# Drawn offsets on the priorities of two mixers, and a memset in place of a transfer of zeros

## The chip, the cores and the metric

The kernel runs on one core of a Trainium2 chip. The metric is the device time of one execution in microseconds; the median of the runs counts. Five engines work side by side, each through its own instructions in order: TensorE (PE in the profile; PEld are its weight loads), VectorE (DVE), ScalarE (ACT), GpSimd (POOL) and SyncE (SP), which here issues the transfers.

## The reference

Two layers of a model of width 1024 run on one sequence of 256 tokens. Each layer is feed-forward, mixer, feed-forward, each followed by a layer norm over the scaled residual:

```python
for layer in range(DEPTH):
    i = layer // 2
    h = layer_norm(DEEPNORM_ALPHA * h + 0.5 * swiglu(h, ffn_w_in[layer, 0], ffn_w_out[layer, 0]), ...)
    if layer % 2 == 0:
        mix = hybrid_mixer(h, ...)
    else:
        mix = nsa_mixer(h, positions, ...)
    h = layer_norm(DEEPNORM_ALPHA * h + mix, ...)
    h = layer_norm(DEEPNORM_ALPHA * h + 0.5 * swiglu(h, ffn_w_in[layer, 1], ffn_w_out[layer, 1]), ...)
```

`hybrid_mixer` projects the tokens and runs two branches: a gated delta rule with 8 value heads, whose chunks need the solution of a triangular system, and a state space scan with 16 heads; both are gated, normalised and projected back. `nsa_mixer` is attention with 16 heads in 2 groups, over compressed, selected and windowed keys.

## The kernel before

The kernel is first written down as a plan and then ordered. Every call such as `nc.vector.tensor_tensor` appends an operation to `self.plan.ops` (`Plan.add`), with the tiles that it reads and writes, its dependences on earlier operations (two accesses of one PSUM bank of which one writes are always kept in order) and a priority: its place in the list, `op.prio = op.idx + self.base`. `Plan.order` then walks through time with a list of ready operations for each engine. On each engine it takes the operation that can start first by prices written out in `Plan.price`, and among those that could start at once the one of lowest priority. Tiles are given their buffers as they are first written; there are two "ps" banks, two "mp" banks and four "acc" banks of PSUM, four "raw" buffers for arriving weights, and 36 tiles of 128x1024 floats for the rest. `K.copy` leaves it to this walk whether ACT or DVE makes a copy. `Plan.emit` issues the operations in the order found, which is why every line of the profile is L534, the line that emits.

Float32 products are made of three matmuls of a rounded kind: a weight tile `raw` is split into a rounded part `whi` and the rest `wlo` (`split`), and `mm3` multiplies high by high, high by low and low by high. Weight splits are most of the work of DVE and much of that of ACT. Small products, transposes (against `ident`) and the inverse run as plain float32 matmuls.

The six stages (feed-forward, hybrid, feed-forward, feed-forward, NSA, feed-forward) are planned one after the other in `run`. Inside the hybrid stage five generators are woven by `weave`, which always continues the one that has made least progress by planned PE time: `delta` (the delta rule and its inverse), `space` (convolutions), `gate`, `space2` (the scan) and `out_a` (the output projection of the first half). The NSA stage weaves `attention`, `dense` (projections of queries, keys and values), `compressed` and `out_g0`. So the place of an operation in the list is the place at which its generator was continued.

The inverse of the triangular system is in `delta`. Sixteen chunk matrices of 64x64 a half partition are inverted by levels: the diagonal blocks of 16 rows by VectorE (`sw`, `Ab`, `W`), then level 4 joins them to blocks of 32 and level 5 to blocks of 64. For a level, `X` times `AT` is masked and written to the columns `half(Tt, 0)` of the tile T (`Tt`, 16 matrices of 64 columns a partition); `Y` and T give the products that are subtracted from `Y` and `X`. At level 4 `half(Tt, 0)` are columns 0 to 15 and 32 to 47 of each 64, at level 5 columns 0 to 31. The products read all 64 columns of T, so between the levels columns 32 to 47 have to be zero again. `zero` does that for the whole tile with a transfer from a tile of zeros, issued on SyncE:

```python
self.nc.sync.dma_start(H3(t, n), self.zeros[:, None, :].to_broadcast([P, n, P]))
```

T and the two `Y` tiles are also cleared this way once ahead of the levels.

Of the kernel before, what the change touches and what calls it, by code (L numbers as in the profile page):

```python
# [40 lines left out]
NSA_SB = (("acc",), ("acc",), ("ps",), ("ps",))  # L41
CATCH = 1
ZERO_AT = 8

ENDS = 3

# [6 lines left out]
def H3(t, h):  # L53
    return t.rearrange("p (h t) -> p h t", h=h)
# [503 lines left out]
class K:  # L558
# [556 lines left out]
    def hybrid(self, x, then):  # L1115
        self.arena = None
        nc, i = self.nc, self.i
# [97 lines left out]
        for n, src in enumerate((kT, qT)):  # L1215
            sq = H3(self.m4(1024, "sq"), 4)
            nc.scalar.activation(sq, src, AF.Square)
            for h in range(4):
                o, c = n * 4 + h, h % 2
# [29 lines left out]
        def delta():  # L1249
# [40 lines left out]
            for j in range(15):  # L1290
# [3 lines left out]
                V.tensor_tensor(W[:, j + 1:, :j + 1], W[:, j + 1:, :j + 1], u, OP.subtract)  # L1294
                if j == ZERO_AT:
                    late = _Gate(self.plan, len(self.plan.ops) - 1)
# [5 lines left out]
            X, Tt = (H3(self.m4(1024, n, "D"), 16) for n in ("X", "T"))  # L1302
# [19 lines left out]
            for lev in (4, 5):  # L1322
                n = 1 << lev
                nb = 32 // n
                half = lambda t, q: t.rearrange("p h (j two i) -> p h j two i", two=2, i=n)[:, :, :, q, :]
                packed = lambda ps: ps.rearrange("p (h j i) -> p h j i", j=nb, i=n)
                m = lm[:, lev - 4, :].rearrange("p (j i) -> p j i", i=n)
                yield
                pT = self.bank("acc")
                for b, h, cp, k in heads:  # L1330
                    nc.tensor.matmul(pT[cp, k * 32:(k + 1) * 32], AT[b][cp, h, cp], half(X, 0)[cp, k], start=True, stop=True)
                V.tensor_tensor(half(Tt, 0), packed(pT), m[:, None].to_broadcast([P, 16, nb, n]), OP.mult)
                yield
                pX, pY = self.bank("acc"), self.bank("acc")
                for b, h, cp, k in heads:
                    nc.tensor.matmul(pY[cp, k * 32:(k + 1) * 32], Tt[cp, k, :], half(Ys[b][cp, :, cp], 1)[:, h],
                                     start=True, stop=True)
                for b, h, cp, k in heads:
                    nc.tensor.matmul(pX[cp, k * 32:(k + 1) * 32], Ys[b][cp, h, cp], half(Tt, 0)[cp, k], start=True, stop=True)
                for b, Y in enumerate(Ys):  # L1340
                    for cp in CP:
                        y = half(Y[cp, :, cp], 1)
                        V.tensor_tensor(y, y, packed(pY[cp, b * 256:(b + 1) * 256]), OP.subtract)
                V.tensor_tensor(half(X, 0), half(X, 0), packed(pX), OP.subtract)
                if lev < 5:
                    self.zero(Tt)

            yield
            pT = [self.bank("acc") for b in range(2)]
# [59 lines left out]
            for b, d in enumerate(blk):  # L1409
                tb = slice(b * P, (b + 1) * P)  # L1410
                attnT, vn = d['attnT'], d['vn']
                o = H3(self.m4(1024, f"o{b}"), 8)
# [138 lines left out]
        def out_a():  # L1551
# [3 lines left out]
            for s in range(4):  # L1555
                wo = self.unit_rows(w_out, 2 * s, 2, 0, D)
                for e in range(2):
                    for b in range(2):
                        for c in range(2):
                            cs = slice(c * 512, (c + 1) * 512)  # L1560
                            self.mm3(acc[b][c], self.xb(oT[0], b, 2 * s + e), (wo[e][0][:, cs], wo[e][1][:, cs]),
                                     s + e == 0, False)
                        yield
        self.weave(list(zip((delta(), space(), gate(), space2(), out_a()), W_HYB)))
        terms = []
        for s in range(4):
# [420 lines left out]
    def run(self, stages):  # L1987
        nc = self.nc
        self.ah = [None, None]
        self.first = True  # L1990
        x = self.new_x()

        warm = self.bank("acc")

        def spin(*heads):
            for n in heads:
                nc.tensor.matmul(warm[:, :n * P], self.ones, self.ones[:, None, :].to_broadcast([P, n, P]),
                                 start=True, stop=True)

        tab = self.one([P, 1], "tab")  # L2000
        nc.scalar.activation(tab, self.mhalf, AF.Silu)
        spin(4, 2)
        self.ah = [self.m4(D, f"h{b}", "L") for b in range(2)]

        def load(b, q):
            cs = slice(q * 512, (q + 1) * 512)
            nc.sync.dma_start(self.ah[b][:, cs], self.i['x'][0, b * P:(b + 1) * P, cs])
            self.transpose_half(x, b, self.ah[b], q)

        load(0, 0)  # L2010
        with _Gate(self.plan, len(self.plan.ops) - 3):
            spin(2, 2)
        self.arrivals = [[], [lambda: load(1, 0)], [], [lambda: load(0, 1), lambda: load(1, 1)]]
        for n, (kind, l, j, idx) in enumerate(stages):
            last = n == len(stages) - 1
            state = {}

            def then(b, acc, s, state=state, last=last, l=l, idx=idx):
                if b == 0:
                    state['x'] = None if last else self.new_x()  # L2020
                    state['gb'] = self.ln_params(l, idx)
                self.layer_norm(b, acc, s, state['gb'], state['x'], last)
            if kind == 'ffn':
                self.ffn(l, j, x, lambda b, acc: then(b, acc, 0.5), last)
            elif kind == 'hyb':
                self.hybrid(x, lambda b, acc: then(b, acc, 1.0))
            else:
                self.nsa(x, lambda b, acc: then(b, acc, 1.0))
            x = state['x']


STAGES = [('ffn', 0, 0, 0), ('hyb', 0, 0, 1), ('ffn', 0, 1, 2), ('ffn', 1, 0, 0), ('nsa', 1, 0, 1), ('ffn', 1, 1, 2)]
# [37 lines left out]
```

## Time and profile before

| what | value |
|---|---|
| median of 3 runs | 1120.43 us (1120.2 to 1120.77) |
| profiled execution | 1120.57 us |
| its span, first to last instruction | 1118.5 us |
| granted TensorE clock | 0.998 |
| PE / PEld / DVE / ACT / POOL busy | 99% / 84% / 79% / 46% / 5% of the span |
| TensorE matmuls | 6545 |
| read from HBM | 194.04 MB, 174 GB/s over the span |

A row of instructions in a timeline reads: start, duration, engine, line, operation, output tile <- input tiles, shapes, count, and in brackets the idle time of the engine ahead of it with what ended it. "Issue" stands for an engine that waited for nothing that the profile shows. Matmuls overlap, and their ends are modelled, so a busy PE is not PE at its peak.

### The profile page before, as it was taken

The page shows a single profiled execution, that of the slowest core. Times are in us where ns is not written, and L with a number is a line of the kernel's source. Part 1 is how long each engine was busy: PE and PEld are TensorE (multiplying, and loading weights), DVE is VectorE, ACT ScalarE, POOL GpSimd, SP SyncE. Part 2 cuts the span into 40 slices and gives each one's busy share as a digit, 9 for nine tenths or more (in the row PEclk, how much of TensorE's full clock was granted, in tenths as well). Part 3 has the DMA queues.
Part 4 walks back from the last instruction along what each step waited for, and adds up shares of the span by engine and source line. Part 5 has one row for each costly group of instructions (what it writes and reads, how often), then busy time and mean ns, then how long its engine had stood idle before and what let it go on. Part 6 is the DMA issues. An engine that isn't in the chain of part 4 may idle for free.

```text
span 1118.5 us, 16483 instructions
## 1 busy us (share of the span) xinstructions
PE 1105.6 (99%) x6545; PEld 943.9 (84%) x6545; DVE 888.5 (79%) x1494; ACT 516.6 (46%) x930; POOL 56.3 (5%) x104
## 2 busy tenths in 40 slices
PE   9999999999999999999999999999999999999997
PEld 7888888899999788888888888888887678888886
DVE  6977768799979999777767977876879989777765
ACT  4635332278736545533423633433346776333320
POOL 1000000012001410000000000000000000000000
PEclk9999999999999999999999999999999999999999
DMA  9876562642933276755564665655426237755511
GB/s 335 302 252 199 183 219 80 188 133 55 271 114 105 85 241 211 263 188 188 189 192 146 236 213 184 201 182 164 150 71 232 76 113 248 242 188 195 181 39 38
DMA packets 148886, 198.37 MB, mean 177 GB/s; under 512 B 9389, under 2 KB 123722, under 8 KB 148810
## 3 DMA queue, kind: packets, MB, share of 16 engines
q1 hardware_dynamic: 148810, 197.33, 53.5%
q8 instruction: 51, 0.84, 0.3%
q14 instruction: 25, 0.20, 0.1%
HBM read 194.04 MB, written 1.05 MB: 174 GB/s over the span
## 4 chain that ended last, share of the span: by engine, by line
PE 87%; DVE 7%; ACT 2%; issue 2%; DMA 1%; POOL 1%; SPq 0%; DVEq 0%; ACTq 0%; POOLq 0%
PE ps L534 52%; PE acc L534 31%; PE mp L534 5%; DVE wlo L534 2%; DVE cv L534 1%; DVE arena L534 1%; DMA raw<-in_nsa_w_in_dram 1%; DVE o L534 0%; POOL arena L534 0%; DMA raw<-in_ffn_w_in_dram 0%; DVE AT L534 0%; ACT P L534 0%; DVE whi L534 0%; DVE y L534 0%; DVE qs L534 0%
## 5 line engine op out<-in xcount | busy, mean ns | idle before, releaser
L534 DVE TENSOR_TENSOR wlo<-raw,whi 128x1024 fp32r<-128x1024 f32 (+2 forms) x351 | 416.3, 1207 | 10.9 <-ACT whi L534 7.7
L534 PE MATMUL ps<-x,whi 128*128 128x512 f32 (+2 forms) x1584 | 369.1, 363 | 1.4 <-ACT cv L534 1.0
L534 PEld LDWEIGHTS ps<-x,whi 128*128 128x128 f32 (+1 forms) x1584 | 278.6, 188 | 46.1 <-ACT cv L534 2.9
L534 ACT ACTIVATE whi<-raw 128x1024 fp32r<-128x1024 f32 (+2 forms) x258 | 258.4, 1045 | 28.2 <-DMA raw<-in_ffn_w_in_dram 17.6
L534 PE MATMUL acc<-whi,g 128*128 128x512 f32 x698 | 228.4, 391 | 0.0
L534 PE MATMUL ps<-x,wlo 128*128 128x256 f32 x1368 | 222.4, 283 | 0.0
L534 ACT ACTIVATE sg<-ps 128x256 f32<-128x256 f32 x156 | 60.0, 385 | 343.4 <-PE ps L534 343.4
L534 PEld LDWEIGHTS ps<-x,wlo 128*128 128x128 f32 x1368 | 197.6, 190 | 11.3
L534 DVE TENSOR_TENSOR sg<-ps,sg 128x256 f32<-128x256 f32 (+1 forms) x158 | 67.4, 427 | 155.6 <-ACT sg L534 154.9
L534 PEld LDWEIGHTS acc<-whi,g 128*128 128x128 f32 x698 | 131.4, 188 | 25.8
L534 PE MATMUL acc<-wlo,g 128*128 128x512 f32 x349 | 136.9, 392 | 0.0
L534 PE MATMUL ps<-whi,x 128*128 128x512 f32 (+1 forms) x480 | 128.6, 385 | 0.0
L534 PEld LDWEIGHTS ps<-whi,x 128*128 128x128 f32 x480 | 85.7, 188 | 15.3 <-issue 0.8
L534 PEld LDWEIGHTS acc<-wlo,g 128*128 128x128 f32 x349 | 65.8, 189 | 10.8
L534 PE MATMUL acc<-whi,x 128*128 128x512 f32 x224 | 74.6, 405 | 0.3 <-DVE x L534 0.2
L534 PE MATMUL ps<-wlo,x 128*128 128x512 f32 (+1 forms) x240 | 67.2, 380 | 0.0
L534 DVE CAST whi<-raw 128x1024 fp32r<-128x1024 f32 (+2 forms) x93 | 63.4, 682 | 4.0 <-DMA raw<-in_nsa_w_in_dram 4.0
L534 PEld LDWEIGHTS acc<-whi,x 128*128 128x128 f32 x224 | 41.6, 188 | 10.3 <-DVE x L534 1.0
L534 PEld LDWEIGHTS ps<-wlo,x 128*128 128x128 f32 x240 | 43.3, 188 | 7.1
L534 POOL TENSOR_TENSOR lnve<-lnve,mhalf 128x1 f32<-128x1 f32 x12 | 11.5, 956 | 735.5 <-DVE lnve L534 735.5
L534 ACT ACTIVATE sg<-sg 128x256 f32<-128x256 f32 x72 | 30.2, 419 | 33.3 <-DVE sg L534 33.1
L534 PE MATMUL acc<-wlo,x 128*128 128x512 f32 x112 | 42.9, 398 | 0.0
(251 smaller groups left out, 1013.1 us busy)
## 6 DMA issues: line engine op xcount, KB each, us to landing
raw<-in_ffn_w_in_dram SPq DMA_DIRECT2D x72, 1024.0 KB, 5.1
raw<-in_ffn_w_out_dram SPq DMA_DIRECT2D x44, 1024.0 KB, 5.1
raw<-in_hyb_w_in_dram SPq DMA_DIRECT2D x20, 1024.0 KB, 5.3
raw<-in_ffn_w_in_dram SPq DMA_DIRECT2D x30, 512.0 KB, 4.9
raw<-in_hyb_w_out_dram SPq DMA_DIRECT2D x8, 1024.0 KB, 5.1
raw<-in_nsa_w_in_dram SPq DMA_DIRECT2D x5, 1024.0 KB, 5.6
raw<-in_nsa_cmp_w_dram SPq DMA_DIRECT2D x4, 1024.0 KB, 5.5
raw<-in_nsa_w_out_dram SPq DMA_DIRECT2D x4, 1024.0 KB, 6.1
```

Source lines behind the costliest of these rows:

```text
L534: r = getattr(getattr(nc, eng), fn)(*[res(a) for a in args], **{k: res(a) for k, a in kw.items()})
```

## The change

A table `ORDER` names two stages, 1 (hybrid) and 4 (NSA), with a seed number, a spread and a run length. `run` notes at which operation each stage begins. After all stages are planned, the operations of those two stages get an offset on their priority: each run of eight consecutive operations shares one draw from a normal distribution, times 3.0. The offsets act in `Plan.order` alone; the list, the dependences and the work stay. Between levels 4 and 5 of the inverse, the transfer over all of T gives way to a memset on GpSimd over columns 32 to 47 of each matrix.

```diff
+ORDER = {
+    1: [(38, 3.0, 8)],
+    4: [(180, 3.0, 8)],
+}
...
                 if lev < 5:
-                    self.zero(Tt)
+
+                    nc.gpsimd.memset(half(Tt, 0)[:, :, 1], 0.0)
...
+        self.marks = []
         for n, (kind, l, j, idx) in enumerate(stages):
+            self.marks.append(len(self.plan.ops))
...
+        ends = self.marks[1:] + [len(self.plan.ops)]
+        for n, terms in ORDER.items():
+            a, e = self.marks[n], ends[n]
+            for number, spread, run in terms:
+                off = np.random.default_rng(number * 10 + n).standard_normal((e - a) // run + 2)
+                for o in range(a, e):
+                    self.plan.ops[o].prio += spread * off[(o - a) // run]
```

## The prediction

> **What bounds the kernel now.** I read the page's shares first, then busy time by stretch, then the waits of TensorE, then the timeline around its holes.
>
> ```profile
> span 1118.5 us, 16483 instructions
> ## 1 busy us (share of the span) xinstructions
> PE 1105.6 (99%) x6545; PEld 943.9 (84%) x6545; DVE 888.5 (79%) x1494; ACT 516.6 (46%) x930; POOL 56.3 (5%) x104
> ```
>
> TensorE (PE) is without work for 1118.5 - 1105.6 = 12.9 us in all. The profiled execution took 1120.57 us, 2.07 us more than its span; the median of the runs, 1120.43, is 0.14 us below it. The three runs differ by 0.57 us; I count 0.2%, 2.24 us, as about what a measurement of this kernel can tell from no change.
>
> Busy time by stretch puts the idle time into stages (columns: busy PE, PEld, DVE, ACT, POOL, then granted clock, DMA share, GB/s). 187 to 460 us is about the first mixer, 794 to 970 the second, 460 to 609 the inside of a feed-forward stage.
>
> ```profile
> 187.00:460.00 273.00, 271.47 (x2056) 240.35 (x2055) 250.22 (x467) 154.49 (x242) 38.10 (x52) 1.00 0.50 159
> 460.00:609.00 149.00, 149.00 (x784) 128.28 (x783) 105.57 (x159) 53.72 (x87) 0.00 (x0) 1.00 0.58 192
> ...
> 794.00:970.00 176.00, 173.75 (x1057) 138.62 (x1056) 151.84 (x276) 108.33 (x277) 10.49 (x26) 1.00 0.48 162
> ```
>
> The feed-forward stretch has no idle PE at all. The mixers, the only stages whose priorities are drawn anew, have 273.00 - 271.47 = 1.53 us and 176.00 - 173.75 = 2.25 us: 3.78 us together. The clock is 1.00 throughout, so no order can gain clock. The rest of the 12.9 us lies at the start and the end of the program, out of the change's reach.
>
> The waits of PE name the holes (who waited for whom: us in total, times, longest):
>
> ```profile
> PE ps L534 <- ACT q L534: 1.3, 1, 1.3
> PE acc L534 <- POOL ones L534: 1.1, 1, 1.1
> PE ps L534 <- ACT cv L534: 1.0, 1, 1.0
> PE mp L534 <- ACT P L534: 0.5, 1, 0.5
> PE mp L534 <- DVE q L534: 0.4, 1, 0.4
> PE mp L534 <- DVE x L534: 0.3, 1, 0.3
> ```
>
> The wait for `ones` is the program's start. The other five lie in the mixers, each happens once, and they add up to 1.3 + 1.0 + 0.5 + 0.4 + 0.3 = 3.5 of the 3.78 us. Each is an accident of order, not a rate that is too low, as the two large ones show. The first, in the hybrid mixer:
>
> ```profile
> 270.90 1.29 ACT L534 ACTIVATE sw<-AT 32x256 f32<-32x256 f32 x2
> ...
> 272.21 0.38 ACT L534 ACTIVATE cv<-ps 128x256 f32<-128x256 f32 x1
> 272.49 0.59 ACT L534 ACTIVATE zs<-ps 128x512 f32<-128x512 f32 x1
> 272.65 0.30 PEld L534 LDWEIGHTS ps<-x,whi 128*128 128x128 f32 x2 [1.46 <-ACT cv L534]
> ```
>
> Two copies that gather the inverse's diagonal blocks stand on ACT ahead of the copy that empties a projection bank; both "ps" banks are full, and PE waits. Had the `cv` copy gone first, it would have run 1.29 us earlier, more than the hole. The second, in the NSA mixer:
>
> ```profile
> 871.55 0.51 ACT L534 ACTIVATE P<-acc,arena 128x256 f32<-128x256 f32 x1
> ...
> 872.00 0.64 ACT L534 ACTIVATE q<-ps 128x512 f32<-128x512 f32 x1
> ...
> 872.69 0.19 PEld L534 LDWEIGHTS ps<-fixed 128*128 128x128 f32 x1 [1.52 <-ACT q L534]
> ```
>
> Here the copy of the queries that empties the bank stands behind the attention's exponentials, and frees it at 872.64, just before PE goes on.
>
> **The change, part by part.** *The T edit.* It removes one transfer of zeros over the whole of T (half a megabyte by the tile's 128x1024 floats), and adds one memset of 16 x 16 = 256 floats a partition. What the transfer held up is read from SyncE's queue, its landing (issue to landing, min/median/max of T's two transfers) and the timeline of the second level of the inverse:
>
> ```profile
> 312.67 0.60 SPq L534 DMA_DIRECT2D T<-zeros  x1
> 319.89 0.37 SPq L534 DMA_DIRECT2D raw<-in_hyb_w_out_dram  x1
> ```
> ```profile
> DMA to landing us min/median/max: 4.0/6.6/9.1
> ```
> ```profile
> 314.62 2.06 PE L534 MATMUL acc<-X,AT 64*64 64x32 f32 x64
> ...
> 316.76 0.69 DVE L534 TENSOR_TENSOR T<-acc,arena 128x512 f32<-128x512 f32 x1 [2.58 <-PE acc L534]
> ...
> 318.74 2.06 PE L534 MATMUL acc<-Y,T 64*64 64x32 f32 x64
> ```
>
> Of the two landings only 4.0 us fits the second transfer, since T is written behind it: 312.67 + 4.0 = 316.67. PE finishes the products that feed T at 314.62 + 2.06 = 316.68. The write at 316.76 waits for both alike, so without the transfer it still starts at 316.76: gain zero. On SyncE's queue the next entry is 7.2 us later, so taking 0.60 us of issue away brings no weight forward that the trace shows to be late.
>
> The memset has no row of its kind. The nearest:
>
> ```profile
> L534 POOL MEMSET mz<- 128x512 f32 x1 | 0.5, 522 | 0.0
> ...
> L534 POOL MEMSET X<- 128x64 f32 x1 | 0.2, 206 | 0.0
> L534 POOL MEMSET ones<- 128x128 f32 x1 | 0.2, 204 | 0.3 <-POOLq L2057 0.3
> ```
>
> Along the line of the contiguous pair (128 floats 204 ns, 512 floats 522 ns) 256 floats take 204 + 318/3 = 310 ns; at the rate of the strided row (64 single floats in 206 ns) 824 ns. I take 310, since its runs are 16 floats long. It waits for the same readers as the transfer, so it starts near 312.7 and ends between 313.0 and 313.5, over 3 us before the write of T, which need not wait for it (it writes other columns), and over 5 us before the products at 318.74, which must. If that cover were gone it would cost at most the 0.8 us. Queued behind it on GpSimd:
>
> ```profile
> 331.43 1.34 POOL L534 TENSOR_SCALAR_AFFINE_SELECT bm<-arena 128x512 fp32r<-128x512 f32 x2 [71.07 <-PE acc L534]
> ```
>
> GpSimd has been idle for 71 us there, so nothing waits behind the memset. Sum for the T edit: 0, from -0.1 to +0.8.
>
> *The offsets.* They add no instruction and remove none. Blocks of eight consecutive operations get a common normal offset of 3 places, so two blocks move against each other by 3 x 1.41 = 4.2 places, typically. Data dependences stay, so PE's work stays the same, and what can change is idle time and the price of turns between kinds of matmul. Idle time: the five holes each hang on which of two neighbours goes first, so a shift of a few places can undo them, -3.5 us at most; it can make new ones of the same kind. I take the five to go and one of the middle size, 0.5, to come: -3.0 us. I lean to a gain because PE had ready work at all but a handful of places among 2056 + 1057 matmuls: a shift of four places rarely empties two banks at once, while each hole that is there stands exactly on such a pair. SyncE's loads are in the shifted blocks too; no hole above was ended by a transfer, so I cost their movement at nothing, the cover being the four raw buffers; without it a hole would be of the kind priced under the slower rival. The price of turns: the weight loads wait without a releaser for
>
> ```profile
> PEld mp L534 <- issue: 9.5, 27, 0.8
> PEld acc L534 <- issue: 5.1, 17, 0.5
> ```
>
> 14.6 us in 44 places, 0.33 us each. Ten places more or fewer are 3.3 us either way; I take none in the sum, and use it as the bound.
>
> The sum against the profiled execution: 1120.57 - 3.0 + 0 = 1117.57, and as a median, 0.14 lower, 1117.4.
>
> [...]
>
> **The rivals.** *Fewer turns as well.* The holes close and ten turns go: 1117.4 - 3.3 = 1114.1. [...] Against it: most turns are transposes and fp32 products that the data flow needs one by one.
>
> *The holes only move.* As many new ones come as go, and the time stays within 2.24 us of 1120.4. For it: the draw is blind. Against it: the rarity of holes.
>
> *Slower: VectorE is late and both projection banks stay full.* The place is the hybrid mixer between 270 and 300 us:
>
> ```profile
> 270.00:300.00 30.00, 28.98 (x228) 27.40 (x226) 29.94 (x80) 22.04 (x40) 0.00 (x0) 1.00 0.72 207
> ```
>
> VectorE is busy 29.94 of 30 us, so a step of the convolutions or of the inverse that falls behind a weight split loses that split's whole time, by the page:
>
> ```profile
> L534 DVE TENSOR_TENSOR wlo<-raw,whi 128x1024 fp32r<-128x1024 f32 (+2 forms) x351 | 416.3, 1207 | 10.9 <-ACT whi L534 7.7
> ```
>
> 1.2 us a time. It decides from the point where both "ps" banks wait at once and no other matmul is ready, as at 272.65. Three such places on top of those of today are +3.6 us: 1124.0. For it: VectorE has no slack here. Against it: ACT is busy only 22.04 of 30 us and most copies can go to either engine.
>
> *The change does nothing.* The offsets are too small to swap neighbours: 1120.4, part of the case "holes only move".
>
> **How the numbers follow.** Chances: forecast 0.42 (1115.4 to 1118.2), fewer turns as well 0.10, holes only move 0.27, slower 0.21. So faster by over 0.2% is 0.42 + 0.10 = 0.52, within it 0.27, slower 0.21. The likeliest is the forecast, 1117.4. The range begins at 1114.0, with the fewer turns at their full price, and reaches to 1122.8, into the slower case as far as two places (1120.4 + 2 x 1.2); beyond the two ends I leave less than 0.2.
>
> **What would show it.** Right: the second `T<-zeros` is gone, a memset of T of about 0.3 us stands near 312 us, and the write of T still comes right behind its products; the feed-forward stretches keep their length; PE's waits for ACT `cv` and ACT `q` are gone or below 0.5 us, and PE's busy time hardly moves. Wrong: new PE waits for ACT or VectorE in the mixers that add up to 3 us or more, or equal idle time with a changed sum of "issue" waits, in which case the turns and not the holes decide. If the span moves while the mixers' idle time and turns stay, the whole picture is wrong.

## The result, and the profile after

| kernel | median | runs | ratio to before |
|---|---|---|---|
| before | 1120.57 us (1120.2 to 1121.37) | 21 | |
| after | 1118.92 us (1118.26 to 1119.56) | 21 | 0.9985, 95% interval [0.9979, 0.9991] |

The change saves 1.65 us, clear of zero and inside the 0.2% that the prediction called no change. The profiled execution of after took 1119.32 us, 0.4 us above its median; its NSA stage, 153.79 us, is the longest of the four traces with the same order in that stage (152.95 to 153.79 us).

The page's shares, and busy time by stage of after (columns as in the prediction; the stretches run from the last product of one feed-forward output projection to the first of the next):

```profile
span 1117.6 us, 16493 instructions
...
PE 1103.3 (99%) x6545; PEld 944.5 (85%) x6545; DVE 886.5 (79%) x1491; ACT 519.9 (47%) x937; POOL 55.3 (5%) x103
```
```profile
192.87:460.61 267.74, 265.13 (x2026) 235.68 (x2024) 244.14 (x455) 155.61 (x244) 36.61 (x52) 1.00 0.50 160
801.17:954.96 153.79, 151.62 (x955) 121.93 (x954) 135.58 (x254) 101.36 (x268) 9.04 (x23) 1.00 0.48 163
```

The same stretches of before:

```profile
192.76:459.84 267.08, 265.55 (x2025) 235.41 (x2024) 244.53 (x457) 152.39 (x239) 37.11 (x51) 1.00 0.51 162
800.34:955.99 155.65, 153.40 (x956) 121.43 (x954) 137.05 (x255) 101.20 (x266) 9.57 (x25) 1.00 0.47 158
```

Nearly all that differs is in these two rows. The feed-forward stretches last the same in both kernels (155.53 us, the last one 152.57), and 0.3 us more are spread over the start, the end and the middle. The hybrid stretch grew by 0.66 us: idle PE went from 267.08 - 265.55 = 1.53 to 2.61 us. The NSA stretch shrank by 1.86 us, and not by idle time, which went from 2.25 to 2.17: PE's busy time fell from 153.40 to 151.62. The waits of PE in after:

```profile
PE mp L539 <- DVE x L539: 1.1, 1, 1.1
PE acc L539 <- POOL ones L539: 1.1, 1, 1.1
PE ps L539 <- ACT cv L539: 1.0, 1, 1.0
PE mp L539 <- DVE arena L539: 0.8, 1, 0.8
PE ps L539 <- ACT q L539: 0.7, 1, 0.7
PE mp L539 <- DVE qT L539: 0.4, 1, 0.4
```

The hole at ACT `cv` stands as it was; the one at ACT `q` halved; those at ACT `P` and DVE `q` are off the list, and new ones of 0.8 us (DVE `arena`) and 0.4 us (DVE `qT`) have come; the one at DVE `x`, 0.3 before, is 1.1. Its timeline, first before, then after:

```profile
378.35 1.09 ACT L534 ACTIVATE x<-mp 128x512 fp32r<-128x512 f32 x2 [2.65 <-PE ps L534]
...
380.24 0.66 PE L534 MATMUL mp<-ident,xT 128*128 128x128 f32 x4 [0.34 <-DVE x L534]
```
```profile
378.02 0.60 ACT L539 ACTIVATE x<-mp 128x512 fp32r<-128x512 f32 x1 [2.40 <-PE ps L539]
...
379.61 0.68 DVE L539 CAST x<-mp 128x512 fp32r<-128x512 f32 x1
...
380.21 1.27 DVE L539 TENSOR_TENSOR x<-mp,x 128x512 fp32r<-128x512 f32 x2
...
380.94 0.66 PE L539 MATMUL mp<-ident,xT 128*128 128x128 f32 x4 [1.14 <-DVE x L539]
```

In before ACT made both rounded copies of a transposed block; here it made one, and the other fell to DVE, which began it 1.59 us later and had the subtractions behind it to do as well. PE waited 0.8 us longer.

A sign of where the busy time of the NSA stage went is at the weight loads that wait without a releaser. Of after, in that stretch:

```profile
PEld mp L539 <- issue: 6.9, 22, 0.8
PEld acc L539 <- issue: 2.7, 9, 0.4
...
PEld ps L539 <- issue: 0.8, 1, 0.8
```

and of before:

```profile
PEld mp L534 <- issue: 8.0, 21, 0.8
PEld acc L534 <- issue: 2.5, 9, 0.4
PEld ps L534 <- issue: 1.8, 3, 0.8
```

12.3 us became 10.4. A *sitting* below is an unbroken row of matmuls on a part of the array (such as the value products of 64 columns and the compression's products of 32). Counted in the order of the trace, the NSA stage has 11 sittings before and 9 after: once two rows of value products have joined, and once the products with the compressed values (`vbd`) follow the value products at once, where before whole-array work stood between.

The T edit did what it says:

```profile
312.16 0.31 POOL L539 MEMSET T<- 128x256 f32 x1 [51.71 <-PE acc L539]
```

### The profile page after: what moved, and what is told of

Read it like the earlier page. It is cut to its first block, busy times and chain, and to the rows that moved or that the text cites. A ratio compares the mean times of both kernels' runs of the same rounds, so it can differ in the third digit from the quotient of the medians.

```text
span 1117.6 us, 16493 instructions
## 1 busy us (share of the span) xinstructions
PE 1103.3 (99%) x6545; PEld 944.5 (85%) x6545; DVE 886.5 (79%) x1491; ACT 519.9 (47%) x937; POOL 55.3 (5%) x103
## 4 chain that ended last, share of the span: by engine, by line
PE 88%; DVE 7%; ACT 3%; DMA 1%; issue 0%; SPq 0%; DVEq 0%; ACTq 0%
PE ps L539 53%; PE acc L539 31%; PE mp L539 5%; DVE wlo L539 2%; DVE cv L539 1%; DVE arena L539 1%; ACT whi L539 1%; DMA raw<-in_nsa_w_in_dram 1%; ACT L539 1%; DMA h<-in_x_dram 0%; ACT sw L539 0%; DVE whi L539 0%; DVE o L539 0%; ACT cv L539 0%; DVE x L539 0%
## 5 line engine op out<-in xcount | busy, mean ns | idle before, releaser
L539 POOL TENSOR_TENSOR lnve<-lnve,mhalf 128x1 f32<-128x1 f32 x12 | 11.5, 956 | 732.2 <-DVE lnve L539 732.2
```

The lines of the kernel that those rows point to most:

```text
L539: r = getattr(getattr(nc, eng), fn)(*[res(a) for a in args], **{k: res(a) for k, a in kw.items()})
```

## The experiments

Theory A: each stage's draw acts in its own stage, the NSA draw gains by fewer and shorter turns, the hybrid draw loses by a hole, the T edit does nothing. Rival B: the T edit made the hybrid stretch longer. Rival C, the prediction's own: holes decide. Stage lengths are those between the feed-forward stages, as above.

**The T edit alone.** Against after:

```diff
 ORDER = {
-    1: [(38, 3.0, 8)],
-    4: [(180, 3.0, 8)],
 }
```

> The T edit alone, no offsets. Theory A (each draw acts in its own stage, the T edit does nothing): the hybrid stretch between the feed-forward stages stays at 267.08 us and the NSA stretch at 155.64 us, the median within 0.3 us of before. Rival B (the T edit is what made the hybrid stretch 0.66 us longer, through a memset that waits on GpSimd or an X that comes late): hybrid 267.7 us, time +0.6 us.

Measured: 1120.43 us, ratio 1.0001 [0.9992, 1.0009]; hybrid 267.06, NSA 155.41 us. Nothing, as theory A has it; B falls.

**The hybrid offsets alone.**

```diff
 ORDER = {
     1: [(38, 3.0, 8)],
-    4: [(180, 3.0, 8)],
 }
...
-                    nc.gpsimd.memset(half(Tt, 0)[:, :, 1], 0.0)
+                    self.zero(Tt)
```

> The offsets of the hybrid stage alone, with the transfer of zeros kept. Theory A: the hybrid stretch grows from 267.08 to about 267.7 us with the hole of 1.1 us ahead of the transposes of xT, NSA stays at 155.64 us, time +0.6 us. Rival B: hybrid at or below 267.08 us, time 0 to -0.5 us, since the loss came with the T edit.

Measured: 1125.75 us (1121.1 to 1132.53), ratio 1.0039 [1.0022, 1.0056]. Both theories missed this. The eleven executions differ by 11 us: three at a mean granted clock of 0.998 took 1121.1 to 1121.65 us, two at 0.999 took 1122.9 and 1123.16, and six at 0.990 to 0.996 took 1125.75 to 1132.53. The profiled execution is one of the six, of 1127.59 us, with a hybrid stretch of 274.51 us. First the weights in before's queue, then, of this run, SyncE's queue, the landing of T's two transfers, the second write of T, and the clock:

```profile
309.24 0.37 SPq L534 DMA_DIRECT2D raw<-in_hyb_w_out_dram  x1
```
```profile
310.62 0.37 SPq L538 DMA_DIRECT2D raw<-in_hyb_w_out_dram  x1
312.07 0.61 SPq L538 DMA_DIRECT2D T<-zeros  x1
```
```profile
DMA to landing us min/median/max: 7.8/8.1/8.4
```
```profile
319.98 0.69 DVE L538 TENSOR_TENSOR T<-acc,arena 128x512 f32<-128x512 f32 x1 [4.46 <-DMA T<-zeros]
...
320.73 3.23 PE L538 MATMUL acc<-Y,T 64*64 64x32 f32 x60 [2.02 <-DVE T L538]
```
```profile
315.00:320.00 5.00, 3.71 (x68) 3.21 (x64) 0.54 (x2) 0.99 (x2) 0.00 (x0) 1.00 0.38 117
320.00:325.00 5.00, 4.27 (x84) 4.27 (x86) 3.17 (x5) 0.42 (x1) 0.00 (x0) 0.60 0.42 121
325.00:330.00 5.00, 5.00 (x61) 4.93 (x59) 2.37 (x5) 0.00 (x0) 0.00 (x0) 0.50 0.23 92
330.00:335.00 5.00, 5.00 (x60) 4.59 (x59) 0.69 (x1) 0.59 (x1) 0.00 (x0) 0.88 0.01 3
```

With the new order a megabyte of weights is issued 1.45 us ahead of the zeros (3.4 us in before, where the zeros go out at 312.67). The zeros land 7.8 us after their issue in place of 4.0: of the two landings only this one fits, since DVE writes T at 319.98. DVE's write of T waits for the transfer, and PE stands for 2.02 us. Then its clock falls to half: 5 x (0.40 + 0.50 + 0.12) = 5.1 us of full clock lost in three rows. The two executions near 1123 us, at full clock, have no trace; their time is what a hole of 2 us alone would give.

**The same, with the weights held back.** As the run before, and:

```diff
                 if lev < 5:
                     self.zero(Tt)
+                    self.zeroed = len(self.plan.ops) - 1
...
-                wo = self.unit_rows(w_out, 2 * s, 2, 0, D)
+                with _Gate(self.plan, self.zeroed if s == 0 else None):
+                    wo = self.unit_rows(w_out, 2 * s, 2, 0, D)
```

> The hybrid offsets with the transfer of zeros kept, as in the run of 1125.75 us, but the first weights of the output projection wait until the zeros over T have landed. Theory A (under the new order a megabyte of weights is issued 1.45 us ahead of the zeros, the zeros land behind it, the write of T waits for them, TensorE stands for 2.0 us and its clock falls to half): the zeros land some 4 us after their issue, the wait for the write of T and the drop of the clock go, the hybrid stretch is near 267.7 us and the time near 1121.3 us, as with the memset. Rival (the hybrid order itself is bad there, or the zeros are slow without the weights): hybrid stays at 272 to 275 us and the time at 1124 us or more.

Measured: 1120.99 us (1120.7 to 1121.45), ratio 1.0006 [0.9997, 1.0015]; hybrid 267.80 us, at a granted clock of 1.00:

```profile
311.74 0.61 SPq L538 DMA_DIRECT2D T<-zeros  x1
312.44 7.21 SPq L538 DMA_DIRECT2D raw<-in_hyb_w_out_dram  x2
```
```profile
316.30 0.69 DVE L538 TENSOR_TENSOR T<-acc,arena 128x512 f32<-128x512 f32 x1 [2.24 <-PE acc L538]
```

The edit does less than was written of it: the weights do not wait until the zeros have landed, they only go out 0.70 us behind them in place of 1.45 us ahead. That is enough. T is written when its products are done, 4.6 us after the zeros were issued. So it was the weights ahead of the zeros; the hybrid order itself costs 0.7 us. Against this run the one above has 2.03 us more idle and 4.68 us more busy PE, the clock's share.

**The NSA offsets alone**, with the transfer (first run) and with the memset (second run). Against after:

```diff
 ORDER = {
-    1: [(38, 3.0, 8)],
     4: [(180, 3.0, 8)],
 }
```

and in the first run alone

```diff
-                    nc.gpsimd.memset(half(Tt, 0)[:, :, 1], 0.0)
+                    self.zero(Tt)
```

> The offsets of the NSA stage alone, with the transfer kept. Theory A: NSA falls from 155.64 to about 153.8 us, the idle time of TensorE in it stays near 2.2 us, and the time is 1.8 us below before, lower than with the whole change. Rival C (my prediction's: the gain is holes of TensorE that close): the idle time in NSA would have to fall by the 1.8 us.

> The NSA offsets and the T edit, no hybrid offsets. Theory A: hybrid 267.1 us and NSA 153.8 us, the time 1.8 us below before and 0.2 to 0.7 us below the whole change. Rival B: hybrid 267.7 us, so no better than the whole change.

Measured: 1117.84 us, ratio 0.9978 [0.9969, 0.9986], and 1118.08 us, 0.9977 [0.9969, 0.9986]. Both are faster than before. Their medians are 0.8 to 1.1 us below that of the whole change too, with ratio intervals that overlap its own; by stage, the hybrid stretch is back at 267.11 and 267.02 us. NSA is 152.95 and 153.30 us:

```profile
800.43:953.38 152.95, 151.58 (x956) 121.92 (x955) 135.62 (x255) 101.45 (x268) 9.07 (x23) 1.00 0.47 164
```
```profile
801.32:954.62 153.30, 151.69 (x955) 121.93 (x954) 135.61 (x254) 101.51 (x268) 9.06 (x23) 1.00 0.47 164
```

Busy time is 151.6 to 151.7 as in after; idle time is 1.37 and 1.61 us, and 2.17 in after, though every engine has its instructions of this stage in the same order in all three. So the busy part, 1.8 us, comes with the order; idle time gives up to 0.9 us more and differs from run to run. The new hole at DVE `arena`, 0.8 us in after, is 0.2 us or less in the other two.

**Fewer sittings by hand.** The kernel before, with one wait moved:

```diff
             po = self.bank(("acc", "mp")[g])
             first = True
+            yield from wait(("c", g, b))
             for r in range(2):
...
-            yield from wait(("c", g, b))
-            yield
             for n in range(4):
```

> The kernel before, with one edit by hand in the NSA stage: each head group waits for its compressed probabilities ahead of its value products, so that the products with the compressed values can follow them at once. In the written order TensorE then changes to part-array matmuls 8 times in that stage in place of 11 (9 with the whole change). Theory A (turns into and out of part-array work are what the NSA draw saved): NSA shorter than 155.64 us, by 1.5 to 2.7 us, with idle time as before, if the earlier wait costs nothing. Rival C (holes): NSA moves with the idle time of TensorE, whatever the number of turns.

Measured: 1121.9 us, ratio 1.0013 [1.0004, 1.0022]; NSA 156.72 us.

```profile
800.32:957.04 156.72, 154.26 (x956) 124.12 (x954) 136.34 (x252) 102.75 (x267) 9.57 (x26) 0.98 0.46 158
870.00:880.00 10.00, 7.57 (x33) 5.95 (x32) 9.63 (x23) 7.93 (x33) 0.60 (x2) 0.70 0.01 2
880.00:890.00 10.00, 10.00 (x73) 6.80 (x72) 5.40 (x13) 5.05 (x14) 0.00 (x0) 0.96 0.32 106
```

Eight sittings, and yet slower; theory A's shorter stage did not come. The holes of PE in the row from 870 us:

```profile
871.06 0.66 PE L534 MATMUL mp<-ident,q 128*128 128x128 f32 x4 [0.33 <-POOL q L534]
872.46 0.30 PE L534 MATMUL mp<-ident,arena 128*128 128x128 f32 x1 [0.75 <-DVE arena L534]
873.51 1.56 PE L534 MATMUL mp<-arena,qT 128*128 128x32 f32 x8 [0.75 <-ACT arena L534]
875.67 1.09 PE L534 MATMUL mp<-ident,P 128*128 128x128 f32 x4 [0.61 <-DVE arena L534]
```

The granted clock is 0.70 in that row and 0.96 in the next: 10 x 0.30 + 10 x 0.04 = 3.4 us of full clock lost. Without that the busy time would be near 150.9 us, an estimate from these rows that counts all of it as slower work.

**The NSA offsets on all but TensorE's operations** (with the T edit, without the hybrid offsets).

```diff
                 for o in range(a, e):
-                    self.plan.ops[o].prio += spread * off[(o - a) // run]
+                    if self.plan.ops[o].eng != 'tensor':
+                        self.plan.ops[o].prio += spread * off[(o - a) // run]
```

> The T edit and the NSA offsets, put on all operations but those of TensorE. The written order has the same 9 part-array sittings as the whole change. Theory A: busy time of TensorE in NSA 151.6 us as with the whole change, against 153.4 before; the idle time may differ, since the loads and copies go in another order. Rival C: the busy time stays at 153.4 us, and what changes is idle time.

Measured: 1121.67 us, ratio 1.0013 [1.0004, 1.0022]; NSA 156.59 us, nine sittings.

```profile
PE ps L538 <- ACT q L538: 2.7, 1, 2.7
```
```profile
870.00:880.00 10.00, 7.13 (x31) 4.51 (x31) 9.68 (x22) 8.10 (x33) 1.71 (x4) 0.83 0.37 119
```

The hole at ACT `q` grew from 1.3 to 2.7 us and the granted clock of that row is 0.83, 10 x 0.17 = 1.7 us of full clock lost. Busy time 153.42 less 1.7 is 151.7, as in after. Here theory A has the busy part and rival C the outcome. That TensorE's own priorities need no offset for nine sittings fits a rule of `Plan.order` which stands above the priorities: as long as a product on a part of the array could start at once, no other is taken (`turn_pen`). A sitting ends when none is ready, and the offsets change what is ready.

**The price of a sitting.** In each of the 72 inner steps of the feed-forward loops a product that no output uses, on a part of the array or on the whole.

```diff
                 self.split(g[0], g[1], sg)
+                z = self.bank("mp")
+                nc.tensor.matmul(z[:64, :64], self.ident[:64, :64], self.ident[:64, :64], start=True, stop=True)
```
```diff
                 self.split(g[0], g[1], sg)
+                z = self.bank("mp")
+                nc.tensor.matmul(z[:, :64], self.ident, self.ident[:, :64], start=True, stop=True)
```

> The kernel before, with one small matmul of 64 rows by 64 columns on a part of the array added in each step of the inner feed-forward loops (78 in all or fewer; no output uses it). These stages have no idle TensorE, so the added time over the number is the price of one part-array matmul with its turn in and out. Theory A: the NSA draw saved two sittings and about 1.8 us, so a turn in and out costs 0.3 us or more above the same product on the whole array: over 0.4 us for each. Rival: turns are cheap, 0.1 us as for any small product.

> The same as the one with part-array matmuls, with a whole-array float32 matmul of 128 rows by 128 columns and 64 moving columns in the same place. By both theories about 0.11 us for the matmul and 0.1 to 0.2 us for the change of kind, for each; theory A has the part-array version dearer by 0.2 us or more, the rival has them alike.

Measured: 1140.62 and 1136.88 us, with spans of 1138.9 and 1134.8 us, so (1138.9 - 1118.5) / 72 = 0.28 us for each on a part, product and turns together, and 0.23 us on the whole array. Under the 0.4 us that theory A wanted: two sittings fewer are worth about 0.6 us by this, a third of the 1.8. The starts of successive matmuls say more: take each interval of the NSA stage less idle time and less the typical interval of that form, and after has about 1.0 us less than before at the borders of part-array work. The remaining 0.8 us lie among the whole-array products of the attention; behind the products of `mm3` the intervals add up to the same within 0.1 us. What shortens those 0.8 us is not shown.

**Holes of known length.** The kernel before, with one hole in each feed-forward stage, of 6, 10, 14 and 20 memsets that the order prices at next to nothing (the lines for this price are left out here); no output uses the products.

```diff
+                if s == 6 and e == 0:
+                    z = self.bank("mp")
+                    nc.tensor.matmul(z[:, :64], self.ident, self.zeros[:, :64], start=True, stop=True)
+                    for _ in range(HOLES.pop(0)):
+                        nc.gpsimd.memset(self.zeros, 0.0)
...
+                    nc.tensor.matmul(z[:, :64], self.ident, self.zeros[:, :64], start=True, stop=True)
```

> The kernel before, with one artificial hole on TensorE in the middle of each of the four feed-forward stages, which have none: a small product waits for a row of GpSimd memsets (6, 10, 14, 20 of them, about 0.2 us each) that the order does not know of; no output uses it. If a hole costs only its length (prediction's rule), the four stages of 155.53 us grow by about 1.2, 2.0, 2.9 and 4.1 us plus 0.5 us for the two products, at a clock of 1.00. If a hole from about 2 us on also takes the clock down, the later ones grow by several us more, and the granted clock of that stretch is below 1.

Measured: 1139.26 us in the profiled execution, 1136.79 us in the only other one. The four holes' wait of PE (sum, times, longest), and the four places, 15 us each:

```profile
PE mp L540 <- POOL zeros L540: 10.4, 4, 4.4
```
```profile
105.00:120.00 15.00, 14.06 (x79) 11.97 (x79) 9.49 (x14) 3.88 (x7) 1.28 (x6) 1.00 0.66 216
532.00:547.00 15.00, 13.02 (x64) 10.82 (x63) 8.34 (x12) 3.50 (x6) 2.10 (x10) 0.89 0.55 187
724.00:739.00 15.00, 11.94 (x54) 9.70 (x53) 7.17 (x12) 4.35 (x8) 2.89 (x14) 0.89 0.43 140
1038.00:1053.00 15.00, 10.63 (x47) 8.71 (x46) 5.57 (x9) 2.78 (x5) 4.14 (x20) 0.77 0.48 162
```

| hole | its stage grows by | growth less the hole |
|---|---|---|
| 0.94 us | 1.69 us | 0.75 us |
| 1.98 us | 4.33 us | 2.35 us |
| 3.06 us | 5.41 us | 2.35 us |
| 4.37 us | 7.22 us | 2.85 us |

The first row has the price of the two products; from 1.98 us on there are 1.6 to 2.1 us more, at a granted clock of 0.89 and 0.77. A hole of two microseconds costs nearly twice its length in this execution. The other one was 2.5 us shorter, at a mean granted clock of 0.996 in place of 0.993, so some of the falls of the clock did not come there; it has no trace to say which. By the granted clock of the rows, 15 x 0.11 = 1.65 us of full clock were lost at the second hole and again at the third, 15 x 0.23 = 3.45 us at the fourth (its stage's growth shows 2.1 of them), and none at the first.

**Other draws**, on the whole change.

```diff
-    1: [(38, 3.0, 8)],
+    1: [(10, 3.0, 8)],
```
```diff
-    1: [(38, 3.0, 8)],
-    4: [(180, 3.0, 8)],
+    1: [(6, 3.0, 8)],
+    4: [(21, 3.0, 8)],
```

> The whole change with another draw for the hybrid stage (number 10 in place of 38). Theory A (a draw is a lottery for its own stage; the NSA stage keeps its gain): NSA 153 to 153.8 us as before with this draw; the hybrid stretch comes out anywhere between 266 and 269 us, with its idle time. Best guess 267.0 us and a time of 1117.9 us. Rival: offsets on the hybrid stage always cost, 267.7 us again.

> Other draws for both stages (6 for hybrid, 21 for NSA). The NSA order again has 9 part-array sittings. If the number of sittings carried the gain, NSA is near 153.5 us; if the small waits and holes carry it, NSA can come out at 155 to 160 us. Hybrid 267 to 269 us. Time 1120 to 1126 us by the lottery.

Measured: 1119.1 us, ratio 0.9988 [0.9979, 0.9997], hybrid 268.07 and NSA 153.05 us; and 1124.8 us, 1.0040 [1.0026, 1.0053], hybrid 270.73 and NSA 156.43 us. My 267.0 us for draw 10 was too low. Its hybrid stretch has the idle time of before, 1.53 us; the whole loss of 1.0 us is busy time, 266.54 us against 265.55, at full clock and with as many sittings as before (13):

```profile
193.00:461.07 268.07, 266.54 (x2025) 235.44 (x2024) 245.70 (x459) 150.67 (x237) 38.85 (x52) 1.00 0.50 160
```

So busy time moves with the order there as well, and the count of sittings does not tell by how much. In the second:

```profile
804.07:960.50 156.43, 153.23 (x956) 123.41 (x954) 138.21 (x256) 99.81 (x263) 10.29 (x27) 0.99 0.47 160
870.00:880.00 10.00, 7.28 (x42) 6.45 (x42) 10.00 (x25) 10.00 (x36) 0.62 (x2) 0.83 0.33 106
```

Nine sittings again; at a granted clock of 0.83 from 870 to 880 us, 153.23 - 10 x 0.17 = 151.5 us of busy time at full clock, and 3.20 us idle. The gain in busy time is there, and idle time and the clock take more than that away. All three hybrid draws (267.7, 268.1, 270.7) are behind the order without offsets (267.1).

## Why the prediction was right or wrong

**What bounds the kernel: right.** PE was full outside the mixers (in after busy for 154.67 of the 155 us from 30 to 185 us, and without a gap from 462 to 616, 617 to 799 and 957 to 1110 us), and the change touched nothing outside them.

**The T edit: right as a sum, wrong in its bounds.** The memset took 312 ns (310 predicted) and the edit alone measures 1.0001. The step that failed is that the write of T "waits for both alike" was taken for a property of the kernel; it was a near tie of before's order. Under the hybrid offsets the zeros behind the weights cost about 4.8 us by the medians (1125.75 less 1120.99; 0.1 to 11.5 us by the single executions), and with the memset the hybrid stretch is 267.74 in place of 274.51 us. Both draws with the transfer kept were not run, so this is put together from the parts. I had priced the two parts of the change one by one, and not the edit under the new order.

**Idle time: the step that failed in the sum.** I took -3.0 us, five holes gone and one come. The hole at `cv` did not move, the one at `x` grew from 0.3 to 1.1, the one at `q` halved; in the two stages idle time went from 3.78 to 4.78 us. The reasoning "a shift of four places rarely empties two banks" treated a hole as something that a shift undoes more easily than makes. Of the five draws measured (three for hybrid, two for NSA) only the NSA draw of the change shortened its stage.

**The price of turns: the term left at nothing.** I quoted two rows (a third, at `ps`, has 2.2 us in 4 places), bounded the term by 3.3 us either way, and took zero. Busy time, where this term stands, decided: 1.8 us less in the NSA stage and 0.4 in the hybrid one, with waits without a releaser in the NSA stage of 10.4 in place of 12.3 us. At full clock (three of the kernels have it after the lost clock of their rows is taken off, an estimate), busy time in the NSA stage is 153.2 to 153.6 us with 11 sittings (seven kernels), 151.5 to 151.7 with 9 (six), about 150.9 with 8 (one). The number goes with the gain. That each sitting costs 0.9 us by its turns is not shown: the probe prices it at 0.3, the borders give about 1.0 of the 1.8 us, and the cause of the rest is open. My sign for this case, equal idle time with a changed sum of these waits, is what the NSA stage shows (2.25 and 2.17 us idle).

**The share of weight loads.** PE's busy share of the NSA stretch is 98.6% in both kernels, while that of the weight loads rose from 78.0% (121.43 of 155.65) to 79.3% (121.93 of 153.79): here the first hid what the second shows.

**The slower rival** had the mechanism by halves. Places where PE runs dry do decide, but at 1.2 us each I priced only the hole. "No order can gain clock" holds here, with a granted clock of 1.00 in both mixers of before, and I did not ask whether an order can lose it: the hole of 2.0 us ran to 6.7 us in the traced hybrid stage.

**The time.** 1118.92 lies in the range, but the forecast of 1117.4 took nearly twice the gain, and that the change came out ahead at all is luck as far as my sum goes: the holes, my -3.0 us, came out at +1.0, and 2.2 us of busy time that I had put at nothing outweighed them. By the time it is the case of holes that only move, to which I gave 0.27, and not the likeliest one. The NSA draw alone has the lowest median, 1117.84 us.

## What to carry to other kernels

When an order is drawn anew, look at what TensorE's busy time contains, not only at its idle time: waits of weight loads without a releaser (10.4 in place of 12.3 us here) and the count of changes between kinds of matmul (9 sittings in place of 11) can show gains that a busy share of 99% hides. Test each part of such a change under the order that the other part makes, since a near tie (a transfer that lands just in time, here after 4.0 us under one order and 7.8 under the other) is no property of the kernel. Price a single hole on TensorE at its length only up to the 1.3 us after which the clock stayed at 1.00 here; from two on add a fall of the clock (1.65 us of full clock lost at the hole of 1.98 us, 5.1 at that of 2.02); by the mean clock six of the eleven executions of the hybrid offsets alone had one.

## What the hardware showed that I had not expected

The granted clock fell at 1.98 us without work in a full stretch (0.89 over 15 us), at 2.02 us in the inverse (0.60, 0.50 and 0.88 over 5 us each; why for so long was not tried), and at four holes of 0.33 to 0.75 us, 2.43 us idle in a row of 10 us (0.70). It stayed at 1.00 at 0.94 us, and in before, where 1.3 and 0.5 us lie 2.3 us apart. By their mean clock some executions of a kernel had such a fall where others had not: of the hybrid offsets alone, five stood at 0.998 and 0.999 and six at 0.990 to 0.996. And half a megabyte of zeros took 7.8 us in place of 4.0 with a megabyte of weights issued 1.45 us ahead of it.
